# Moving operands, scalings and gates inside one decoder block: reused weight-block buffers, later output scaling, weight rows split behind the first tokens, and a gated projection that is parked before it is gated

## The chip, the cores and the metric

The kernel is one launch on one core of a Trainium2 chip. The core has a matrix engine (PE), a vector engine (DVE), a scalar engine (ACT), GpSimd (POOL), and sixteen DMA engines. SP issues most of the transfers. Every engine works through its own queue in a fixed order, and one that waits holds up all that stands behind it in that queue. The metric is the device time of one execution in microseconds (us). Three runs of the kernel before gave 1465.24 us in the median (1464.39 to 1468.95).

## The reference

The block takes x (1024 tokens by 1024 channels, float32). What matters here:

```
proj = x @ w_in -> q | f | i | og | pool_v | gate_a | gate_b
a = HGRN2(q, f, i), per-head RMSNorm, * g * sigmoid(og), @ w_a
b = per-group linear(causal_mean(pool_v) - pool_v) * pool_scale
mix = (sigmoid(gate_a) * a + sigmoid(gate_b) * b) @ w_out
x = LN(alpha * x + mix);  x = LN(alpha * x + relu(x @ w_up)^2 @ w_down)
```

HGRN2 is a recurrence over tokens with a forget gate f, eight heads of 128 channels. Its lower bound for f is made from `lb_logits` with a softmax over two rows. RMSNorm divides each head's output by the root of its mean square. The full float32 accuracy of the products is kept by splitting operands.

## The kernel before, in words

**Products.** Each operand is split into a high part (ACT casts it to the fast matrix format) and a low part (DVE subtracts the high part from the original). A product of two split operands is three matmuls. The large products use a seven-product scheme on 2 by 2 blocks (Strassen's, in Winograd's form): of a weight the blocks b11, b12, b21, b22 and the sums T1 to T4 are needed, of the tokens the blocks a11, a12, a22 and the sums s1 to s4. `pair` (line 267) issues seven steps. Each step prepares one weight operand (`w_part`, line 245, which casts on ACT, line 126, and subtracts on DVE, line 127) and then runs one product of twelve 128x512 matmuls (`prod`, lines 212 to 215). Operand tiles come from a ring of ten, that is, five operands ahead.

T3 = b22 - b12 (line 284), T2 = T3 + b11 (line 301), T4 = b21 - T2 (line 309), T1 = b22 - T2 (line 316). T3 has a tile of its own, `t`. T2 is written over b11, T1 over b12, T4 over b21. `loaded_blocks` (line 231) takes five tiles of a ring of six for each pair, in the order b11, b21, t, b12, b22, and issues the four loads on SP (line 223). So the next pair's b21 takes the buffer of this pair's b11, its b12 that of this pair's `t`, its b22 that of this pair's b12.

**First stage.** The value columns i of `w_in` are made first, from x as it arrives. `first_tokens("a11", ...)` (line 183) transposes x on PE, four row blocks kp of the operand, and splits them (line 131 on ACT, line 132 on DVE). `parts(b11)` (line 559) splits the four row blocks of the weight. The few instructions of the lower bound stand ahead of that (lines 440 to 449).

**Recurrence.** Sixteen halves (eight heads, two halves of the tokens) run as `turns` between the products of the other projections: after every product, one turn. A half has 8 or 9 turns (`PER_HALF`). In turn 0 `outputs` (line 1010) loads the sigmoid of og (tile `og`, one buffer, line 1012), makes the output in one PSUM bank, squares it on ACT (line 1022), takes the root (ACT, line 1023) and the reciprocal (DVE, line 1024), and at once scales four chunks on ACT (line 1026). At `TURN_BACK`, turn 4, `turn_outputs` transposes the scaled output, multiplies by og on DVE (line 1034) and sends it to DRAM: plain writes on SP (lines 636, 638) and writes that add, issued by GpSimd (line 640). `states` and the next load of v stand in the same turn.

**The projection by w_a.** Four column pairs p. In its first half (p = 0, 1) the operands `o` and `s` are loaded from DRAM (line 618) and split (lines 131, 132) while the products run. The second half (p = 2, 3) uses the split operands again. Each of the four results of a pair goes to a `take`: `gated` (line 1116) loads a gate tile (tag `ga`, twelve buffers) and a tile of b (tag `gb`, two buffers), multiplies (DVE, line 1120), adds (DVE, line 1121), and for p >= 2 splits the sum for the product by `w_out` (line 121); for p < 2 it is parked and split in the second half (`unpark`). Rows of `w_out` pass through `gb` too (line 1146). Then `mix` (line 1227) multiplies by `w_out`, normalises (GpSimd adds the last term, line 1199), and the MLP follows with the same `pair`.

**Order.** A planner lays down each queue's order ahead of the run, from program order, priorities and its own estimates of durations. During the recurrence PE keeps the program's order. `issue_after` puts the instructions of a block behind a named one on the same engine.

## Time and profile before

| What | Value |
| --- | --- |
| Median of three runs | 1465.24 us |
| The profiled execution | 1466.59 us |
| Its span, first to last instruction | 1464.9 us |
| PE, DVE, ACT, POOL busy | 1435.5, 1100.1, 759.0, 107.6 us |
| Mean granted PE clock | 0.996 |
| Moved by DMA | 228.15 MB, mean 156 GB/s |

Read it so. PE's records overlap, since matmuls are pipelined: a 128x512 matmul is recorded with about 0.39 us and yet they start about 0.23 us apart. So a stretch in which PE is "busy" throughout can be told from one that runs at full rate by counting matmuls. A row of the windows view has the stretch, its length, and for every engine busy time and number of instructions, then the granted clock, the DMA share and GB/s. In a timeline the bracket at the end of a row tells how long the engine sat idle before it and what ended that.

### The profile page before, as it was taken

Reading aid. Unit: us, or ns where it says so; the run is one execution under the profiler, and the core shown is the slowest. Engines: PE = TensorE matmul, PEld = TensorE weight load, DVE = VectorE, ACT = ScalarE, POOL = GpSimd, SP = SyncE. Lnnn points to the kernel's source line nnn. Section 1 sums busy time; section 2 is a strip of 40 time slices with the busy share of each in tenths; the row PEclk is TensorE's granted clock in tenths of the full one; section 3 lists DMA queues with packets and bytes.
Section 4 is the critical chain, followed back from the end, with each engine's and each line's share of the span. In section 5 each row is a group of like instructions: output and inputs, shape, how many; then the busy total and the mean of one; then the engine's idle time right before and its main releaser. Section 6 shows DMA issues by size and latency. Waiting matters only on the chain.

```text
span 1464.9 us, 20840 instructions
## 1 busy us (share of the span) xinstructions
PE 1435.5 (98%) x7377; PEld 1188.4 (81%) x7377; DVE 1100.1 (75%) x1807; ACT 759.0 (52%) x1383; POOL 107.6 (7%) x288
## 2 busy tenths in 40 slices
PE   8999999999999999999999999999999999999997
PEld 7788888788878888877788878888888888888886
DVE  4967886796797796477985598666666787777977
ACT  5545566655755655555542366555556443333435
POOL 0002011211211210000002100000000100000000
PEclk9999999999999999999999999999999999999999
DMA  7142245345435546788673135444447774445422
GB/s 259 58 137 87 73 126 169 80 134 155 109 87 146 142 116 184 211 300 286 204 232 113 61 99 180 144 154 148 157 148 261 280 262 142 166 132 170 129 72 115
DMA packets 187161, 228.15 MB, mean 156 GB/s; under 512 B 12176, under 2 KB 110512, under 8 KB 187056
## 3 DMA queue, kind: packets, MB, share of 16 engines
q1 hardware_dynamic: 181088, 212.91, 43.9%
q0 software_dynamic: 5184, 11.54, 4.0%
q10 hardware_dynamic: 784, 2.38, 0.5%
q8 instruction: 58, 0.95, 0.3%
q14 instruction: 47, 0.39, 0.1%
HBM read 149.70 MB, written 77.07 MB: 155 GB/s over the span
## 4 chain that ended last, share of the span: by engine, by line
PE 87%; DVE 6%; DMA 4%; issue 1%; ACT 1%; SPq 0%; DVEq 0%; POOL 0%; ACTq 0%
PE ps_pj L212 15%; PE ps_pj L215 14%; PE ps_pj L214 14%; PE ps_pj L1412 4%; PE ps_pj L1413 4%; PE ps_pj L1411 4%; PE ps_pj L114 2%; PE ps_pj L113 2%; PE ps_pj L115 2%; PE ps_tr L1412 1%; PE ps_tr L1413 1%; PE ps_tr L1411 1%; PE ps_sc L215 1%; DVE w L127 1%; PE ps_hg L215 1%
## 5 line engine op out<-in xcount | busy, mean ns | idle before, releaser
L212 PE MATMUL ps_pj<-act,w 128*128 128x512 f32 x1068 | 420.2, 395 | 10.8 <-ACT c L275 3.3
L215 PE MATMUL ps_pj<-act,w 128*128 128x512 f32 x1068 | 415.7, 391 | 1.3 <-DVE w L127 1.3
L214 PE MATMUL ps_pj<-act,w 128*128 128x512 f32 x1068 | 415.0, 390 | 0.0
L126 ACT CAST w<-raw 128x512 fp32r<-128x512 f32 x310 | 192.5, 622 | 278.1 <-PE ps_pj L214 201.7
L127 DVE TENSOR_TENSOR w<-raw,w 128x512 fp32r<-128x512 f32 x310 | 212.1, 686 | 92.8 <-ACT w L126 87.6
L212 PEld LDWEIGHTS ps_pj<-act,w 128*128 128x128 f32 x1068 | 200.7, 188 | 56.9 <-ACT c L275 4.6
L215 PEld LDWEIGHTS ps_pj<-act,w 128*128 128x128 f32 x1068 | 200.8, 188 | 45.2 <-DVE w L127 2.6
L214 PEld LDWEIGHTS ps_pj<-act,w 128*128 128x128 f32 x1068 | 200.8, 188 | 40.8 <-DVE act L132 0.2
L1373 ACT CAST act<-act 128x1024 fp32r<-128x1024 f32 x66 | 66.9, 1050 | 109.0 <-issue 35.0
L279 DVE TENSOR_TENSOR c<-c,ps_pj 128x512 f32<-128x512 f32 x95 | 64.8, 682 | 39.1 <-PE ps_pj L215 35.6
L1374 DVE TENSOR_TENSOR act<-act,act 128x1024 fp32r<-128x1024 f32 x66 | 79.5, 1220 | 18.5 <-ACT act L1373 17.4
L1413 PE MATMUL ps_pj<-act,act 128*128 128x512 f32 x240 | 93.0, 389 | 0.0
L1412 PE MATMUL ps_pj<-act,act 128*128 128x512 f32 x240 | 93.0, 389 | 0.0
L1411 PE MATMUL ps_pj<-act,act 128*128 128x512 f32 x240 | 92.5, 389 | 0.0
L275 ACT COPY c<-ps_pj 128x512 f32<-128x512 f32 x96 | 55.8, 581 | 3.1 <-issue 1.8
L284 DVE TENSOR_TENSOR raw<-raw,raw 128x512 f32<-128x512 f32 x43 | 29.6, 690 | 33.2 <-DMA raw<-in_w_in_dram 28.8
L1411 PEld LDWEIGHTS ps_pj<-act,act 128*128 128x128 f32 x240 | 45.0, 188 | 9.4
L1412 PEld LDWEIGHTS ps_pj<-act,act 128*128 128x128 f32 x240 | 45.0, 188 | 9.4
L1413 PEld LDWEIGHTS ps_pj<-act,act 128*128 128x128 f32 x240 | 45.0, 188 | 9.3
L1282 ACT ACTIVATE c<-c 128x512 f32<-128x512 f32 x61 | 38.5, 632 | 1.7
L1281 ACT ACTIVATE c<-c 128x512 f32<-128x512 f32 x46 | 29.1, 632 | 15.0 <-DVE c L279 15.0
L1367 DVE TENSOR_TENSOR act<-act,ps_pj 128x512 f32<-128x512 f32 x45 | 30.1, 682 | 6.0 <-PE ps_pj L1413 5.7
(416 smaller groups left out, 2680.5 us busy)
## 6 DMA issues: line engine op xcount, KB each, us to landing
h<-c SPq DMA_DIRECT2D x106, 256.0 KB, 2.7
raw<-in_w_in_dram SPq DMA_DIRECT2D x100, 256.0 KB, 3.3
act<-h SPq DMA_DIRECT2D x78, 256.0 KB, 3.0
draw<-in_w_down_dram SPq DMA_DIRECT2D x16, 1024.0 KB, 7.6
raw<-in_w_up_dram SPq DMA_DIRECT2D x56, 256.0 KB, 2.8
hf<-h SPq DMA_DIRECT2D x34, 256.0 KB, 3.0
s<-og POOLq DMA_DIRECT2D x28, 256.0 KB, 6.1
v<-v SPq DMA_DIRECT2D x16, 256.0 KB, 3.3
```

Source lines behind the costliest of these rows:

```text
L126: A.copy(hi, src)
L127: V.tensor_sub(lo, src, f(hi))
L212: PE.matmul(ps, wh[:, k], th, start=first and k == 0, stop=False, skip_group_check=True)
L214: PE.matmul(ps, wh[:, k], tl, start=False, stop=False, skip_group_check=True)
L215: PE.matmul(ps, wl[:, k], th, start=False, stop=k == CH - 1, skip_group_check=True)
L275: A.copy(t, ps)
L279: V.tensor_add(t, t, ps)
L1373: A.copy(hi, src)
L1374: V.tensor_sub(lo, src, f(hi))
L1411: PE.matmul(ps, hh[:, w], wh, start=fresh and n == 0, stop=False, skip_group_check=True)
L1412: PE.matmul(ps, hh[:, w], wl, start=False, stop=False, skip_group_check=True)
L1413: PE.matmul(ps, hl[:, w], wh, start=False, stop=n == M - 1, skip_group_check=True)
```

## The change

Five things are changed.

- In `pair`, T2 is written over b12 in place of b11, and T1 over T3's tile in place of b12.
- `outputs` stops at the reciprocal. The four scalings are issued two turns later (`scale_outputs`, `TURN_SCALE` = 2), behind the latest cast of a weight operand on ACT. `TURN_BACK` is 5, so `turn_outputs`, `states` and the load of v come one turn later.
- At the start only rows 0 and 1 of b11 are split ahead of the tokens. Row 2 is split behind the token block kp = 1, row 3 behind kp = 3, on both engines. The lower bound's instructions are issued behind the last split of a11.
- In the first half of the projection by w_a results are parked as they come (`park`), with no gate: the parked tiles are the rooms of the pair, eight buffers, and the fourth result is copied out of PSUM by ACT. Their gates and b tiles are loaded in the second half (`gate_parked`), u = 0 ahead of its first step, u = 1 behind it. `ga` has four buffers in place of twelve.
- The gating runs on GpSimd, but for the results that lie in PSUM (one per pair of the second half), which stay on DVE.

The diff, cut to its core:

```diff
 PER_HALF = 8.5
-TURN_BACK = 4
+TURN_BACK = 5
+TURN_SCALE = 2
...
-    made_last, made_hi = {}, {}
+    made_last, made_hi, made_kp = {}, {}, {}
...
         xp[name][kp] = act_tile()
-        made_last[name], made_hi[name] = (i.ins for i in split_into(xp[name][kp], src))
+        made_last[name], made_hi[name] = made_kp[name, kp] = [i.ins for i in split_into(xp[name][kp], src)]
...
+    last_hi = [None]
...
     def w_part(src):
-        return split(src, w_tile)
+        hi, lo = w_tile(), w_tile()
+        last_hi[0] = A.copy(hi, src).ins
+        V.tensor_sub(lo, src, f(hi))
+        return hi, lo
...
-    def pair(raw, rooms, takes, pz_tag="pj", twin=False, pc_tag="pj", turned=False):
+    def pair(raw, rooms, takes, pz_tag="pj", twin=False, pc_tag="pj", turned=False, into=None):
...
-        def added(t, ps):
-            V.tensor_add(t, t, ps)
-            return t
+        def added(t, ps, to=None):
+            to = t if to is None else to
+            V.tensor_add(to, t, ps)
+            return to
...
                 make_t2()
-            return w_part(b11)
+            return w_part(b12)
...
             if turned:
-                minus_sum(b11, c["t"], b11)
+                minus_sum(b12, c["t"], b11)
             else:
-                V.tensor_add(b11, c["t"], b11)
+                V.tensor_add(b12, c["t"], b11)
...
             if turned:
-                minus_sum(b21, b11, b21)
+                minus_sum(b21, b12, b21)
             else:
-                V.tensor_sub(b21, b21, b11)
+                V.tensor_sub(b21, b21, b12)
...
             if turned:
-                minus_sum(b12, b22, b11)
+                minus_sum(c["t"], b22, b12)
             else:
-                V.tensor_sub(b12, b22, b11)
-            return w_part(b12)
+                V.tensor_sub(c["t"], b22, b12)
+            return w_part(c["t"])
...
             with tc.high_priority(PRIO):
-                takes[0](added(c[11], ps["c"]))
+                takes[0](added(c[11], ps["c"], into and into()))
...
             with tc.high_priority(PRIO):
-                takes[1](ps["a"])
+                takes[1](copied(into, ps["a"]) if into else ps["a"])
...
         e01 = const.tile([P, 16], F32, name="e01")
-        V.tensor_max(lb, prm[:, 0:8], prm[:, 8:16])
...
-        V.tensor_scalar_mul(g_neg, g_col, -1.0)
...
         first_tokens("a11", "tr", "tr", "hg", "hg")
-        w = parts(b11)
+        w = parts(b11[:2])
+        for row, kp in zip(b11[2:], (1, 3)):
+            lo_done, hi_done = made_kp["a11", kp]
+            with tc.issue_after(lo_done), tc.issue_after(hi_done):
+                w += parts([row])
+        with behind_parts("a11"):
+            V.tensor_max(lb, prm[:, 0:8], prm[:, 8:16])
+            V.tensor_sub(e01[:, 0:8], prm[:, 0:8], lb)
+            V.tensor_sub(e01[:, 8:16], prm[:, 8:16], lb)
+            A.activation(e01, e01, AF.Exp)
+            V.tensor_add(lb, e01[:, 0:8], e01[:, 8:16])
+            V.reciprocal(lb, lb)
+            V.tensor_mul(lb, lb, e01[:, 0:8])
+            V.tensor_scalar(one_lb, lb, -1.0, 1.0, ALU.mult, ALU.add)
+            g_neg = e01[:, 0:8]
+            V.tensor_scalar_mul(g_neg, g_col, -1.0)
...
                 V.reciprocal(ss, ss)
-                for c in range(CH):
-                    A.activation(on[:, chunk(c)], o[:, chunk(c)], AF.Copy, scale=ss[:, c : c + 1])
+                self.o, self.root = o, ss
...
+            def scale_outputs(self):
...
+                with tc.issue_after(last_hi[0]):
+                    for c in range(CH):
+                        w = chunk(c)
+                        A.activation(self.on[:, w], self.o[:, w], AF.Copy, scale=self.root[:, c : c + 1])
...
                 for turn in range(1, round(at) - round(at - PER_HALF)):
+                    if turn == TURN_SCALE and old:
+                        old.scale_outputs()
...
         def mg_tile(tag, bufs):
-            return lambda: (pk[0] if tag == "ga" else mg).tile([P, HALF], F32, tag=tag, name=nm(tag), bufs=bufs)
+            return lambda: (pk[0] if tag in ("ga", "park") else mg).tile([P, HALF], F32, tag=tag, name=nm(tag), bufs=bufs)
...
-        def gated(j, u, park):
+        def gated(j, u, in_bank):
...
             def take(src):
-                t = loaded(gad[j][u], mg_tile("ga", 12))
-                V.tensor_mul(t, t, src)
-                V.tensor_add(t, t, loaded(pbd[j][u], mg_tile("gb", 2)))
-                if park:
-                    parked[u, j] = t
-                else:
-                    merged[u][j] = split_act(t)
+                eng = V if in_bank else G
+                t = loaded(gad[j][u], mg_tile("ga", 4))
+                eng.tensor_mul(t, t, src)
+                eng.tensor_add(t, t, loaded(pbd[j][u], mg_tile("gb", 2)))
+                merged[u][j] = split_act(t)
+            return take
...
+        def park(j, u):
+            def take(t):
+                parked[u, j] = t
...
                 raw[0], _ = wide_block(w_a, 0, cols[0], block_tile())
-            room = mg_tile("room", 4)
-            takes = [gated(2 * p + i, u, p < 2) for u in range(2) for i in range(2)]
-            return pair(raw, (c_tile, room, room), takes, "hg", True, turned=True)
...
-        def unpark(*which):
-            for u, j in which:
+            if p < 2:
+                room = mg_tile("park", 8)
+                takes = [park(2 * p + i, u) for u in range(2) for i in range(2)]
+            else:
+                room = mg_tile("room", 4)
+                takes = [gated(2 * p + i, u, (i, u) == (1, 0)) for u in range(2) for i in range(2)]
+            return pair(raw, (c_tile, room, room), takes, "hg", True, turned=True, into=room if p < 2 else None)
...
+        def gate_parked(u):
+            for j in range(CH):
+                t = parked[u, j]
+                G.tensor_mul(t, t, loaded(gad[j][u], mg_tile("ga", 4)))
+                G.tensor_add(t, t, loaded(pbd[j][u], mg_tile("gb", 2)))
...
+        def unpark(u):
+            for j in range(CH):
...
         two = [a_pair(p) for p in range(2, 4)]
-        then = (
-            lambda: unpark((0, 0), (0, 1), (0, 2), (0, 3)), lambda: out_rows_of(0, 1, 2, 3), lambda: out_rows_of(4, 5, 6, 7),
-            lambda: None, lambda: None, lambda: None, lambda: None,
-        )
-        for i, after in enumerate(then):
+        gate_parked(0)
+        for i in range(7):
             run(*(p[i : i + 1] for p in two))
-            after()
-        unpark((1, 0), (1, 1), (1, 2), (1, 3))
+            if i == 0:
+                unpark(0)
+                gate_parked(1)
+            elif i < 3:
+                out_rows_of(*range(4 * i - 4, 4 * i))
+        unpark(1)
```

More of the change, by code (lines that the diff above doesn't have):

```diff
@@ L439, in tile_hybrid_block @@
         e01 = const.tile([P, 16], F32, name="e01")
-        V.tensor_max(lb, prm[:, 0:8], prm[:, 8:16])
-        V.tensor_sub(e01[:, 0:8], prm[:, 0:8], lb)
-        V.tensor_sub(e01[:, 8:16], prm[:, 8:16], lb)
-        A.activation(e01, e01, AF.Exp)
-        V.tensor_add(lb, e01[:, 0:8], e01[:, 8:16])
-        V.reciprocal(lb, lb)
-        V.tensor_mul(lb, lb, e01[:, 0:8])
-        V.tensor_scalar(one_lb, lb, -1.0, 1.0, ALU.mult, ALU.add)
-        g_neg = e01[:, 0:8]
-        V.tensor_scalar_mul(g_neg, g_col, -1.0)
         x_rows = [xr.tile([P, CH, D], F32, name=f"x{u}", bufs=1) for u in range(2)]
```

## The prediction

> **What bounds the kernel now.** I read the page's busy times first, then the windows, then PE's waits, and then the timelines of the places at which PE stands.
>
> ```profile
> PE 1435.5 (98%) x7377; PEld 1188.4 (81%) x7377; DVE 1100.1 (75%) x1807; ACT 759.0 (52%) x1383; POOL 107.6 (7%) x288
> ```
>
> PE is the bound, and no part of the change takes a matmul away. All there is to win is PE's lost time: 1464.9 - 1435.5 = 29.4 us of recorded idleness, and some more inside "busy" stretches. The next rows show where. Columns: stretch, length, busy us and count for PE, PEld, DVE, ACT, POOL, then clock, DMA share, GB/s.
>
> ```profile
> 245.00:325.00 80.00, 76.76 (x524) 63.70 (x523) 65.09 (x137) 49.50 (x113) 14.68 (x43) 1.00 0.39 113
> 425.00:442.00 17.00, 14.24 (x117) 11.41 (x110) 16.97 (x39) 12.61 (x31) 3.98 (x13) 1.00 0.22 66
> 625.00:635.00 10.00, 7.17 (x24) 5.07 (x23) 5.32 (x9) 3.74 (x7) 0.00 (x0) 0.83 0.99 333
> 667.00:708.00 41.00, 37.74 (x162) 29.90 (x161) 31.08 (x51) 22.32 (x42) 0.00 (x0) 1.00 0.87 290
> 708.00:757.00 49.00, 48.75 (x215) 40.07 (x214) 42.69 (x71) 21.85 (x38) 0.00 (x0) 1.00 0.53 167
> ```
> ```profile
> 950.00:975.00 25.00, 25.00 (x112) 20.71 (x111) 16.28 (x25) 13.77 (x24) 0.00 (x0) 1.00 0.45 156
> ```
>
> The last row is the yardstick: a full stretch holds 112 matmuls in 25 us, one per 0.223 us. By it the first half of the projection by w_a (667 to 708) should hold 184 and holds 162: 22 x 0.223 = 4.9 us lost. Its second half (708 to 757) lacks 4.7, 1.0 us. The recurrence's two bad stretches have 3.24 + 2.76 = 6.0 us of idleness. The stretch from 625 lacks 21, 4.6 us, partly through a lower clock (0.83). The start comes below; the tail isn't touched.
>
> **The start.**
>
> ```profile
> 9.76 0.60 PE L170 MATMUL ps_hg<-ident,x 128*128 128x128 f32 x4
> 12.38 0.50 PE L501 MATMUL ps_pj<-w,act 128*128 128x512 f32 x1 [2.02 <-ACT act L131]
> ```
> ```profile
> 10.60 1.14 ACT L126 CAST w<-b 128x512 fp32r<-128x512 f32 x2 [2.12 <-DMA b<-in_w_in_dram]
> 11.64 0.21 ACT L443 ACTIVATE e<-e 128x16 f32<-128x16 f32 x1
> 11.76 1.05 ACT L131 CAST act<-ps_tr 128x512 fp32r<-128x512 f32 x2
> ```
>
> PE has transposed all four token blocks at 10.36, but the first product waits until 12.38 for the tokens' cast. ACT was free from 8.48 (10.60 less 2.12) and stood at the weight rows 2 and 3, whose load had not landed, with the tokens queued behind. With those rows and the exponential behind the tokens, ACT casts blocks 0 and 1 as soon as they are transposed. If PE's queue keeps the transposes ahead of the first product, that starts near 10.4: 2.0 us won. If it starts on block 0 at once, up to 3.2. Rows 2 and 3 are late next: cast from 10.6 on, while blocks 0 and 1 feed PE with 24 matmuls, 5.4 us, to 15.8. That covers two casts and subtractions (about 2.4 us). The ten small instructions of the lower bound go behind the split at no cost; what hides them is the whole first stage, as the first forget gate comes after it. I take -2.0, with ends at +0.5 (a row late once) and -3.2.
>
> **The scalings, two turns later.**
>
> ```profile
> PE ps_pj L212 <- ACT c L275: 3.3, 3, 1.6
> ...
> PE ps_hg L212 <- ACT act L131: 2.1, 1, 2.1
> ```
> ```profile
> 287.94 0.88 ACT L1026 ACTIVATE tH<-ps_hg,ss 128x128 f32<-128x128 f32 x3 [0.41 <-DVE ss L1024]
> 288.71 0.59 ACT L275 COPY c<-ps_pj 128x512 f32<-128x512 f32 x1
> ```
>
> PE's longest wait for a PSUM copy, 1.6 us, is this one: the copy stands on ACT behind three scalings, and these behind the reciprocal on DVE. Without them ACT is free at 287.53 (287.94 less 0.41), and the copy runs 1.2 us earlier. The work remains (four scalings per half, sixteen halves), with ACT at 49.50 of 80 us here. Who waits for it, the transposes, comes three turns later. I take -1.2 for this place and nothing for the others; ends 0 and -2.5, as DVE would be late next.
>
> **T2 over b12, and the turn that sends the output.** Both act on when the next pair's weights can be loaded.
>
> ```profile
> SPq L618 <- DMA s<-og: 50.1, 15, 7.6
> ```
> ```profile
> 277.18 0.34 SPq L618 DMA_DIRECT2D og<-og  x1
> 277.61 0.39 SPq L223 DMA_DIRECT2D raw<-in_w_in_dram  x1
> ```
> ```profile
> 273.91 0.69 DVE L127 TENSOR_TENSOR w<-raw,w 128x512 fp32r<-128x512 f32 x1 [1.07 <-ACT w L126]
> 276.63 0.69 DVE L127 TENSOR_TENSOR w<-raw,w 128x512 fp32r<-128x512 f32 x1 [2.03 <-ACT w L126]
> 280.79 0.69 DVE L284 TENSOR_TENSOR raw<-raw,raw 128x512 f32<-128x512 f32 x1 [3.46 <-DMA raw<-in_w_in_dram]
> ```
>
> DVE stands 3.46 us at T3 for the next pair's b22, and the recurrence's instructions queue behind it. That block's buffer was free at 274.60, when T1's low part (the row of 273.91) was done. But SP stood at the load of og, whose only buffer is read by the adding writes of the half before; this wait occurs 15 times, 50.1 us in all. The load of b22 went out at 277.61, 3.0 late.
>
> After the change b21's buffer is free as soon as T2 is made. b12 gets T3's tile, which now holds T1 to its end, 274.60; b22 gets b12's, free a little before. So both can go at 274.6 to 275.0: b12 later than before, b22 0.4 later than its old bound. By buffers alone T3 gains nothing. What decides is og. Its sending stands one turn later (one product of 12 x 0.223 = 2.7 us): PE's transposes, DVE's product, SP's plain writes, GpSimd's adding writes, the states (their first reader, the next output, comes three turns later) and the load of v. The old order had og's load between b12's and b22's, so the planner held its buffer to be free there. Moved by 2.7 us it should fall behind both. T3 then comes about 2.6 us earlier; with og still ahead, 2.7 later. DVE is full from 425 to 442 (16.97 of 17.00), so part of its waiting comes back on PE. Of the 6.0 us less 1.2 I take 2.0; ends -4.8 and +18.7 (worked out with its rival).
>
> **The first half of w_a, ungated.**
>
> ```profile
> ACT act L131 <- DMA c<-s: 7.3, 8, 2.2
> ACT act L131 <- DMA c<-o: 6.5, 3, 3.4
> ```
> ```profile
> DMA packets 8208, 11.67 MB, mean 292 GB/s; under 512 B 694, under 2 KB 3345, under 8 KB 8204
> ...
> ga<-ga SPq DMA_DIRECT2D x12, 256.0 KB, 5.3
> ...
> gb<-pb SPq DMA_DIRECT2D x4, 256.0 KB, 2.9
> ```
>
> These two views are of 667 to 707. ACT waits 13.8 us for operands from DRAM, and PE's 2.1 us wait above is one of them. Of the 11.67 MB moved, 16 loads of 262,144 bytes, 4.2 MB, are gates and b. At 292 GB/s they are 14.4 us of transfer, mixed into SP's queue between the operands. In the second half all of it meets a DMA share of 0.53. Here 8 products and 8 additions leave DVE, and two PSUM copies (0.59 us each, as the copy above) come to ACT at 22.32 of 41: no cost. Weights and ring waits stay, so of 4.9 us I take -4.0; ends -4.9 and 0.
>
> **The second half, with GpSimd.**
>
> ```profile
> 708.00:757.00 49.00, 7.43 (x11) 1.00 0.53 167
> ```
> ```profile
> 708.00:757.00 49.00, 7.31 (x11) 1.00 0.53 167
> ```
> ```profile
> L1199 POOL TENSOR_TENSOR r<-r,act 128x1024 f32<-128x1024 f32 x6 | 14.4, 2397 | 197.2 <-DVE r L1198 194.3 <-issue 2.9
> ```
> ```profile
> 257.64 0.19 POOL L922 COPY ek<-p 128x4 f32<-128x4 f32 x1
> ...
> 258.20 0.65 POOL L923 COPY ek<-p 128x4 f32<-128x4 f32 x1
> ```
>
> The first two rows are lines 1120 and 1121 alone: 11 multiplications and 11 additions, 14.7 us. Two results, four instructions, 2.7 us, stay on DVE, so it falls from 42.69 to 30.7 of 49. GpSimd gets 14 results, 28 instructions. Half of the 1024-wide row is 1.2 us each, 33.6 in all: it fits, barely. Behind it wait its own rings: 14 more b tiles and 8 rows of `w_out` pass through the two buffers of `gb`, and SP stands at each. The cover is `mix`, whose products for the first four row tiles PE can start on, and 16 of the 28 serve the later tokens. The last two rows are the same copy of four elements, 0.19 us and 0.65 us: GpSimd can be held up beside DVE. Whether DVE is held up by a long GpSimd instruction, no row shows. If it never is, the stretch wins at most its 1.0; if all 33.6 us exclude DVE, it has 64.3 us for 49, 15.3 over. The rows are nearer to GpSimd as the loser, so I take +0.5.
>
> The Trainium skill (SBUF — State Buffer, Who interferes with whom) says that a DVE instruction with two SBUF inputs and a GpSimd one that reads SBUF exclude each other, and that "Issue order, not op shape, decides who blocks." By that rule the 28 instructions may each hold DVE, which is the first rival below; the two copies agree with it from GpSimd's side.
>
> The stretch at 625 gets 0: b22's bound there is as before; ends -4.6 and +2.
>
> **The sum**, against the profiled execution of 1466.59 us (1464.9 us of span and 1.7 around it): -2.0 - 1.2 - 2.0 - 4.0 + 0.5 = -8.7, so 1457.9. The median of the runs stands 1.35 lower: 1465.24 - 8.7 = 1456.5.
>
> **Rivals.**
>
> *DVE is shut out in the second half.* For it: 33.6 us of GpSimd in 49, and the copy of 0.65 us. Against it: DVE falls to 63% there, and only 12 instructions are for the tokens that `mix` needs first. At half of the 15.3 over, +7.6 in place of +0.5: -1.6, 1463.6 us.
>
> *Slower: og's load still stands ahead of the weights.* One mechanism: the later turn frees og 2.7 us later at fifteen places, and T3 comes 2.7 later on DVE, with the recurrence behind it. At the place shown 3.46 us at T3 went with 1.6 us on PE, so 2.7 would cost 1.25, fifteen times 18.7. Then -2.0 - 1.2 + 18.7 - 4.0 + 0.5 = +12.0, 1477.2 us. It decides (slower by 4.4) from 11.1 us, 0.74 per place. Against it: DVE idles 15 of 80 us there, and a whole product has been added between.
>
> *The loads are only moved.* Operands still arrive late, since the weights of the second half and the buffers of `c` hold them, and the gates pile up on `gb`: -1.0 in place of -4.0, +1.0 in place of +0.5: -5.2, 1460.0. Against it: the 14.4 us of transfer stood right among the operands.
>
> *More than I count.* The low clock at 625 comes with the late weights there; if those come in time through the new order, 4.6 more go, and 2 more in the recurrence: -15.3, 1449.9.
>
> **How the numbers follow.** Forecast 0.50, DVE shut out 0.17, og ahead 0.15, only moved 0.10, more 0.08. A measurement of this kernel can tell about 0.3%, 4.4 us. Faster: 0.50 + 0.05 + 0.08 = 0.63. Within: 0.05 from "only moved", 0.13 from "shut out", 0.03 from og = 0.21. Slower: 0.12 + 0.04 = 0.16. The forecast's own range is 1451 to 1461. The range given, 1448 to 1469, leaves out og's case.
>
> **What would show it.** First product near 10.4. No scaling between a reciprocal and a PSUM copy; PE's wait for line 275 in the recurrence gone. SP's wait for og's writes well under 50 us, DVE's before line 284 shorter. No gate load before the second half, and over 178 matmuls in what answers to 667 to 708. GpSimd some 33 us busy in the second half, DVE's instructions still about 0.69 us and not set apart by gaps while GpSimd works. I am wrong if T3's waits grow, or if PE stands between the second half and `mix`.

## The result and the profile after

The changed kernel takes 1478.6 us in the median of four runs (1477.41 to 1479.8), beside 1465.1 us for the kernel before on the same chip. The ratio is 1.0091, 95% interval [1.0075, 1.0108]: 0.9% slower, where 0.6% faster was forecast, and outside the range. The profiled execution has a span of 1477.2 us, 12.3 more than before.

The page's busy times after, and the longest of PE's waits (what waited, on what, us in total, times, longest):

```profile
PE 1441.6 (98%) x7377; PEld 1193.3 (81%) x7377; DVE 1099.0 (74%) x1779; ACT 759.2 (51%) x1385; POOL 149.4 (10%) x316
```
```profile
PE ps_pj L213 <- ACT w L250: 7.0, 1, 7.0
PE ps_pj L213 <- ACT c L281: 5.9, 4, 2.3
PE ps_pj L114 <- DVE ga L1141: 3.3, 1, 3.3
```

The number of matmuls is the same. PE is idle for 35.6 us of the span, beside 29.4 before, and busy 6.1 us longer: half of the 12.3 us is waiting, and half is the same work at a lower pace. GpSimd has 42 us more, for 28 instructions. PE's longest wait is 7.0 us in one place, three times the longest before, and the wait for the PSUM copy in the recurrence, which was to go, has grown from 3.3 to 5.9 us. Where the time is shows best in the windows view, by matmul counts. Of before, the start and the two stretches around the projection by w_a:

```profile
0.00:15.00 15.00, 10.04 (x49) 8.84 (x50) 5.65 (x15) 6.92 (x13) 2.06 (x28) 0.94 0.86 291
15.00:30.00 15.00, 15.00 (x72) 12.51 (x71) 5.83 (x12) 9.30 (x18) 0.00 (x0) 0.95 0.87 306
600.00:675.00 75.00, 71.53 (x304) 57.24 (x303) 52.19 (x82) 38.35 (x68) 2.62 (x3) 0.98 0.84 272
675.00:775.00 100.00, 96.48 (x421) 78.25 (x420) 81.72 (x133) 45.31 (x81) 0.00 (x0) 1.00 0.73 239
```

and of after, with one of the prediction's stretches:

```profile
0.00:15.00 15.00, 12.64 (x63) 11.39 (x64) 6.07 (x14) 8.27 (x15) 2.06 (x28) 1.00 0.86 296
15.00:30.00 15.00, 14.55 (x77) 12.04 (x76) 9.29 (x18) 9.52 (x18) 0.00 (x0) 1.00 0.85 300
245.00:325.00 80.00, 75.44 (x513) 62.83 (x512) 64.13 (x136) 48.67 (x111) 13.80 (x43) 0.98 0.38 105
600.00:675.00 75.00, 67.17 (x280) 53.79 (x279) 47.87 (x77) 36.21 (x70) 2.65 (x3) 0.93 0.84 266
675.00:775.00 100.00, 93.02 (x391) 75.18 (x390) 75.69 (x97) 46.19 (x84) 43.55 (x28) 0.97 0.63 202
```

At 0.223 us a matmul: the start gained 140 - 121 = 19 matmuls, 4.2 us. From 600 to 675 it lost 24, 5.4 us; from 675 to 775 it lost 30, 6.7 us. That makes +7.9 of the 12.3. The stretches do not hold exactly the same work, since the kernel is shifted by some us, so this is a reading to within one or two us. The rest is in the recurrence, where PE idles 4.6 us from 245 to 325 (3.2 before) and the clock is lower. Note the clock column: 0.94 and 0.95 became 1.00 at the start, and 0.98 and 1.00 became 0.93 and 0.97 at the projection. That is where PE's longer work comes from. Apart from the last few us of the span, PE works 19.7 us at half the clock in this execution (five stretches, from 287, 434, 622, 693 and 769), and 6.8 us in the kernel before (two, from 13 and 631). Half of the difference is 6.4 us.

### The profile page after: what moved, and what is told of

Its sections match the earlier page's. It is cut to its first block, busy times and chain, and to the rows that moved or that the text cites. A ratio compares the mean times of both kernels' runs of the same rounds, so it can differ in the third digit from the quotient of the medians.

```text
span 1477.2 us, 20892 instructions
## 1 busy us (share of the span) xinstructions
PE 1441.6 (98%) x7377; PEld 1193.3 (81%) x7377; DVE 1099.0 (74%) x1779; ACT 759.2 (51%) x1385; POOL 149.4 (10%) x316
## 4 chain that ended last, share of the span: by engine, by line
PE 78%; DMA 6%; DVE 6%; issue 5%; ACT 3%; POOL 2%; SPq 0%; DVEq 0%; POOLq 0%; ACTq 0%
PE ps_pj L213 12%; PE ps_pj L215 12%; PE ps_pj L216 12%; PE ps_pj L1446 4%; PE ps_pj L1447 4%; PE ps_pj L1445 4%; PE ps_pj L114 2%; PE ps_pj L115 2%; PE ps_pj L116 2%; PE ps_tr L1446 1%; PE ps_tr L1447 1%; PE ps_tr L1445 1%; PE ps_hg L213 1%; PE ps_hg L215 1%; PE ps_sc L213 1%
## 5 line engine op out<-in xcount | busy, mean ns | idle before, releaser
L250 ACT CAST w<-raw 128x512 fp32r<-128x512 f32 x303 | 188.0, 622 | 272.8 <-PE ps_pj L215 196.2
L291 DVE TENSOR_TENSOR raw<-raw,raw 128x512 f32<-128x512 f32 x43 | 29.6, 688 | 33.0 <-DMA raw<-in_w_in_dram 28.4
L652 POOL DMA_DIRECT2D s<-og x28 | 25.0, 1165 | 145.2 <-DVE og L1052 145.2
```

The source lines that it names most:

```text
L250: last_hi[0] = A.copy(hi, src).ins
```

## The experiments

Theories at this point: (1) the later turn makes the next weights, or the pooled blocks, late; (2) GpSimd's gates and DVE hold each other up; and against both, that the loads of gates and b, now through smaller rings, are what is late. All ratios are to the kernel before on the same chip.

| Kernel | Median, us | Ratio | 95% interval |
| --- | --- | --- | --- |
| start alone | 1460.76 | 0.9963 | 0.9951 to 0.9975 |
| T2 over b12 alone | 1466.96 | 1.0002 | 0.999 to 1.0013 |
| scalings and turn alone | 1479.79 | 1.0091 | 1.0075 to 1.0106 |
| w_a and gates alone | 1476.04 | 1.0065 | 1.0051 to 1.0079 |
| scalings, turn 4 | 1467.1 | 1.0009 | 1.0 to 1.0018 |
| turn 5, old scalings | 1481.6 | 1.0106 | 1.0091 to 1.0121 |
| gates, GpSimd 16 wide (most of the gating left out) | 1467.98 | 1.0015 | 1.0006 to 1.0025 |
| gates, all on DVE | 1464.2 | 0.9992 | 0.9983 to 1.0001 |
| states at 5, sending at 4 | 1467.89 | 1.0018 | 1.0008 to 1.0029 |
| turn 5, writes by GpSimd | 1477.2 | 1.008 | 1.0067 to 1.0093 |
| turn 5, product into tH | 1471.54 | 1.0036 | 1.0024 to 1.0048 |
| turn 5, both | 1475.22 | 1.0052 | 1.0033 to 1.0071 |
| turn 4, product into tH | 1469.62 | 1.0023 | 1.0012 to 1.0033 |
| turn 3 | 1469.87 | 1.0018 | 1.0007 to 1.0028 |
| turn 5 but the last at 4 | 1472.25 | 1.0054 | 1.004 to 1.0067 |
| start, gates on DVE | 1460.83 | 0.9966 | 0.9954 to 0.9979 |
| the same with T2 | 1462.1 | 0.9969 | 0.9953 to 0.9985 |
| all, turn 4, gates on DVE | 1463.27 | 0.9981 | 0.9972 to 0.999 |

### The four parts, each alone

Each of these four kernels is the one before with one part of the diff: the hunks of the start; those of T2, T4 and T1 in `pair`; those of `scale_outputs`, `TURN_SCALE` and `TURN_BACK`; those of `park`, `gated` and `gate_parked`.

> Only the start is changed: weight rows 2 and 3 behind the token blocks, the lower bound behind the split. Theory (the loss is the sum of parts that act where they stand): PE's lost time in the first 75 us, 10.0 us before and 5.9 with all changes, falls by about 4 us here too, and the whole time by 3 to 4.5 us. Rival (a lead won at the start is used up in the recurrence, which stands on other waits): first product equally early, whole time within 1.5 us of before.

> Only T2 over b12 and T1 over T3's tile. Theory (buffers alone move T3's inputs by 0.4 us, and the turn is what costs): within 2 us of before, PE's idle time from 245 to 325 us about 3.2 us as before. Rival (b12 coming 2.5 us later holds DVE at T3): 3 to 6 us slower, with DVE's idle time before the T3 line clearly over 33 us.

> Only the scalings two turns later and the output's turn one later. Theory (the later turn keeps buffers of the recurrence longer, and the loads behind them on SP come late): 6 to 10 us slower, with most of it at 575 to 650 us, where the last turns and the pooled products meet, and some at 250 to 325. Rival (that stall comes from T2's buffers or from the shift of the start): within 2 us of before.

> Only the projection by w_a: first half parked, gates in the second half, GpSimd. Theory (the two-buffer ring of the b tiles and GpSimd make the second half's end late, the first half wins nothing): 6 to 9 us slower, with a stall of some 3 us where mix waits for a gated tile. Rival (the second half is late only since the recurrence before it ended badly, with operands and SP behind): 2 us slower or less, or faster by up to 4 as forecast.

The start gained 5.0 us by the medians, T2 nothing, scalings with the later turn cost 14, the projection's part 10. So two parts carry the loss; I had expected 6 to 10 and 6 to 9 us of them. All four add up to +20, the whole change to +13.5: the parts disturb each other.

The start's trace, PE's timeline:

```profile
9.68 0.60 PE L170 MATMUL ps_hg<-ident,x 128*128 128x128 f32 x4
10.04 0.48 PE L491 MATMUL ps_pj<-w,act 128*128 128x512 f32 x1
```
```profile
0.00:15.00 15.00, 12.36 (x63) 11.12 (x64) 5.87 (x14) 8.23 (x15) 2.06 (x28) 1.00 0.85 294
15.00:30.00 15.00, 14.55 (x78) 12.04 (x77) 9.33 (x18) 9.50 (x18) 0.00 (x0) 1.00 0.86 302
```

The first product stands right behind the last transposes, at 10.04 in place of 12.38. That is 2.3 us. Up to 30 us PE has 20 more matmuls than before, 4.5 us. Most of the other 2.2 us is clock: 0.94 and 0.95 before, 1.00 now. Before, the clock is 0.50 from 13.1 to 16.5, where matmuls start 0.43 us apart; that costs 1.7 us. Before, PE waited twice (1.3 us for x, 2.0 for the tokens' cast); here only once, 1.0 us for x. The Trainium skill (TensorE: Matmul & The Clock Gate, Part 1) says that PE falls to half rate after an idle window of about 3.4 us. The two waits of before come to 3.3 us with only transposes between them, so the rows do not contradict it; which window it was they do not show.

### Scalings or turn?

```diff
-TURN_BACK = 5
+TURN_BACK = 4        # scale_only: the part above with the old turn
```
```diff
-TURN_BACK = 4
+TURN_BACK = 5        # back5_only: kernel before with nothing else
```

> Kernel before with the four scalings moved behind the weight cast of the second turn, the sending of the outputs left at its old turn (4). The two edits of this part together made the kernel 14 us slower. Theory A, the later sending does it (og's buffer comes free a turn later, so the weights behind it are late): this run is between -2.5 and +2 us of before, since only the scalings moved. Theory B, the scalings do it (they now stand on ScalarE behind a cast that itself waits for a load, and the turning of the output waits for them): this run is 8 to 14 us slower. Theory C, it takes both (the scalings fit neither before nor behind the copies): in between.

> Kernel before with the sending of the outputs one turn later (5 in place of 4), the scalings where they were. Theory A, the later sending does it: 8 to 14 us slower, with vector engine waits at T3 or ScalarE waits at the weight cast longer at many of the halves. Theory B, the scalings do it: within 3 us of before. By the order of the queue, if og's load now goes out behind the two weight loads, the single stall of 3.46 us at T3 near 280 should be shorter; if ahead, near 6 us.

The turn does it all: +15.5 us by itself. The scalings are worth +1.3 us, at the edge of what can be measured. And they did not move. ACT's timeline with the scalings two turns later, at the old turn:

```profile
288.18 0.88 ACT L1038 ACTIVATE tH<-ps_hg,ss 128x128 f32<-128x128 f32 x3 [0.41 <-DVE ss L1030]
288.94 0.59 ACT L281 COPY c<-ps_pj 128x512 f32<-128x512 f32 x1
```

The reader is to see the same picture as before: three scalings, then PE's copy. In the whole change it is the same, at 285.82. What releases them is DVE's reciprocal, which stands in DVE's queue behind T3, the scans and a mask; in each of the sixteen halves, here as in the kernel before and in the whole change, the first scaling starts within 0.5 us of the reciprocal's end. A place two turns further on in the program, behind a cast that had already run, was no later place in the queue.

### What in the later turn costs 15 us

```diff
-                    if turn == TURN_BACK:
-                        if old:
-                            old.turn_outputs()
+                    if turn == TURN_BACK - 1 and old:
+                        old.turn_outputs()       # late_states, TURN_BACK = 5
+                    if turn == TURN_BACK:
```
```diff
-            nc.sync.dma_start(out=od[h][u], in_=t)
+            nc.gpsimd.dma_start(out=od[h][u], in_=t)     # back5_pool; osd likewise
```

> The later turn (5 in place of 4) was 15.5 us slower by itself. Here only half of what moved with it is late: the states, the load of v and the piece of the next half's preparation that takes their place are as in that kernel, while the transposes of the output, its product and its writes stay at turn 4. Theory A, the late sending does it (SP stands at og's plain write until the product, with the next weights' loads behind it in its queue): this kernel is within 3 us of before. Theory B, the states or the changed order of the pieces does it: 12 us or more slower.

> Kernel before with the sending, the states and the load of v all at turn 5, but the plain writes of the output issued from GpSimd's queue in place of SP's. Theory A (SP stands at og's write, the weights' loads behind it): most of the 15.5 us goes; what is left is the one stall near 624, where the loads of the pooled blocks wait for the buffers of tH that the outputs now hold longer (some 4 us): 0 to 6 us slower than before. Theory A2, the wait for og's buffer counts as well (og's load still waits for its writes): about 8 us slower. Theory B, states and pieces: 12 us or more slower.

With the states and v late and the sending at its old turn, 2 us are left: the sending does it. With the writes in GpSimd's queue 11.7 us remain, between what I had expected of two theories (about 8, and 12 or more). Two places in the traces show what the later sending does. First, near 250. SP's queue and DVE's T3, before:

```profile
240.07 0.34 SPq L636 DMA_DIRECT2D o<-og  x1
...
249.47 0.43 SPq L223 DMA_DIRECT2D raw<-in_w_in_dram  x1
```
```profile
253.68 0.69 DVE L284 TENSOR_TENSOR raw<-raw,raw 128x512 f32<-128x512 f32 x1 [1.65 <-DMA raw<-in_w_in_dram]
```

and with turn 5 alone:

```profile
243.75 0.34 SPq L636 DMA_DIRECT2D o<-og  x1
244.18 0.38 SPq L709 DMA_DIRECT2D og<-c  x1
244.61 1.53 SPq L638 DMA_DIRECT2D s<-og  x3
246.24 1.61 SPq L223 DMA_DIRECT2D raw<-in_w_in_dram  x2
...
250.22 0.47 SPq L223 DMA_DIRECT2D raw<-in_w_in_dram  x1
```
```profile
255.59 0.69 DVE L284 TENSOR_TENSOR raw<-raw,raw 128x512 f32<-128x512 f32 x1 [2.83 <-DMA raw<-in_w_in_dram]
```

The plain writes of the output fall 3.7 us later, and the first of the next weights' loads, whose buffer is free at 244.3 (DVE's subtraction of 243.64, 0.68 us long), now stands behind the four writes of the output and one other transfer: 1.9 us late. T3 too comes 1.9 us later, and the recurrence's scans stand behind it, but that load is not what it waits for. It waits for b22's, the last in each fence, which goes out 0.2 us behind the subtraction that frees its buffer in both kernels (249.47 and 250.22, subtractions done at 249.31 and 250.05). So 0.75 us are there already at the subtraction; the other 1.2 are the transfer, which lands 4.1 us after its issue before and 5.3 us after it now, with the transfers ahead of it more closely packed. It is not og's load that stands ahead of the weights, as the rival had it, but og's writes; yet over the whole recurrence DVE's waits for weights at T3 come to 30.1 us with turn 5 alone, beside 28.8 before, so T3's waits are not where the 15.5 us come from.

The order that I had forecast did come about. At the place that the prediction shows, near 280, SP's queue and DVE of the whole change:

```profile
270.04 2.21 SPq L224 DMA_DIRECT2D raw<-in_w_in_dram  x2
276.89 0.34 SPq L630 DMA_DIRECT2D og<-og  x1
```
```profile
277.96 0.69 DVE L291 TENSOR_TENSOR raw<-raw,raw 128x512 f32<-128x512 f32 x1 [3.39 <-DMA raw<-in_w_in_dram]
```

og's load stands behind both loads of weights, and still DVE waits 3.39 us at T3, beside 3.46 before. The later of the two loads goes out at 271.88, right behind the subtraction that frees its buffer (done at 271.85), and takes 6.0 us to land, where the load that T3 waited for before took 3.1. From 272 to 277.9 the queue of GpSimd's adding writes fills 50.7% of the DMA engines' time; from 277.6 to 280.7 in the kernel before it moves nothing. So what og's load had waited for, the adding writes, now runs beside the weights. That it slows them is my reading of these rows; no run here tests it alone. With turn 5 alone the order is the same there: T3's wait is 2.54 us, and T3 comes 2.4 us later than before.

Second, near 620, where the pooled blocks `po` are loaded into tH's two buffers, which hold the scaled outputs until PE has turned them. Before (PE, SP, ACT):

```profile
607.74 0.60 PE L1032 MATMUL ps_tr<-ident,tH 128*128 128x128 f32 x4
```
```profile
610.22 0.37 SPq L618 DMA_DIRECT2D tH<-po  x1
```
```profile
614.57 0.62 ACT L126 CAST w<-tH 128x512 fp32r<-128x512 f32 x1 [3.83 <-DMA tH<-po]
```

and with turn 5 alone (PE, SP, ACT, and the windows from 625):

```profile
618.82 0.60 PE L1032 MATMUL ps_tr<-ident,tH 128*128 128x128 f32 x4
```
```profile
619.79 0.39 SPq L223 DMA_DIRECT2D raw<-in_w_in_dram  x1
...
620.82 0.38 SPq L223 DMA_DIRECT2D raw<-in_w_in_dram  x1
...
621.97 0.41 SPq L618 DMA_DIRECT2D tH<-po  x1
```
```profile
629.65 0.62 ACT L126 CAST w<-tH 128x512 fp32r<-128x512 f32 x1 [10.04 <-DMA tH<-po]
```
```profile
625.00:630.00 5.00, 0.00 (x0) 0.00 (x0) 0.00 (x0) 0.35 (x1) 0.00 (x0) 0.79 1.10 277
630.00:635.00 5.00, 4.16 (x10) 3.21 (x11) 3.16 (x5) 2.31 (x5) 0.00 (x0) 0.53 1.03 368
```

The block's load had gone out 2.5 us behind the transposes, ahead of the weights; now it goes out 3.2 us behind, with two weight loads ahead of it, and takes 7.7 us to be used in place of 4.4, at a full DMA share. ACT, which casts in order, stands 10 us, and PE 5.9. Then the clock falls to 0.53, and in the next 5 us PE, busy for 4.16, starts 10 matmuls where that time at full rate holds 18.7: 1.9 us more. By the same section of the Trainium skill (TensorE: Matmul & The Clock Gate, Part 1) a wait over its window of about 3.4 us halves the clock; this row agrees, and the wait of 1.6 us near 287 in the kernel before left the clock at 1.00. But in the whole change a shorter wait, alone, goes before the half clock too (PE, and the window behind):

```profile
287.23 0.78 PE L213 MATMUL ps_pj<-act,w 128*128 128x512 f32 x1 [2.25 <-ACT c L281]
```
```profile
287.28:290.69 3.41, 3.41 (x8) 2.73 (x9) 3.41 (x11) 1.96 (x6) 0.10 (x1) 0.50 0.27 75
```

So do waits of 1.80 us (to 432.8) and 2.11 us (to 692.9) in the same execution, while one of 2.13 us (to 689.3) in the kernel before leaves the clock at 1.00. A wait well under 3.4 us can therefore cost 3.4 us at half the clock; when it does, these runs do not show.

How much is each place?

```diff
-                    if turn == TURN_BACK:
+                    if turn == (5 if n < 16 else TURN_BACK):     # back5_early, TURN_BACK = 4
```

> Kernel before with the sending at turn 5 for all halves but the last, which stays at turn 4. In the traces 7.1 us of PE's extra lost time under the later turn came after 600, most of it one stall of 5.9 us and the low clock behind it, where the load of a pooled block waits until the last outputs are transposed out of tH. If that one place is half of the price, this kernel is 7 to 9 us slower than before. If the places are independent of the last half's turn and the price is spread, 12 us or more; if the last place is all of it, within 3 us.

+6.6 us by the medians, +7.9 by the ratio (turn 5 alone: 15.7 and 15.5). So the last half's turn alone takes some 8 to 9 us, and the fifteen before it 7 to 8, about half a us each. But the place near 620 is eased in this kernel, not mended. The transposes are back at 615.19, and the block's load still goes out at 619.82, since SP stands 3.6 us, until 619.41, at a load of f that waits for a write; ACT stands 9.4 us, PE 3.4 in place of 5.9, and 3.4 us at half the clock follow in place of 6.8. So the release of tH is one part of that place, and SP's other waits are another.

The other question is whether the buffer of og, or SP's standing at its writes, is the price:

```diff
-                V.scalar_tensor_tensor(self.og, pt, gain, self.og, ALU.mult, ALU.mult)
-                put_output(self.h, self.u, self.og)
+                V.scalar_tensor_tensor(self.on, pt, gain, self.og, ALU.mult, ALU.mult)
+                put_output(self.h, self.u, self.on)     # on5 at turn 5, on4 at turn 4, on5_pool with GpSimd's writes
```

> Kernel before with the later turn (5), the output's product written into the tile of the scaled outputs (tH) in place of og's own, so that og's buffer is free when the product is made and not when its writes have landed; SP still stands at the plain write ahead of the weights' loads. Of the 15.5 us of the later turn, GpSimd's queue for the plain write took back 4. If og's buffer is the rest, this kernel comes to +4 to +8 us; if neither (tH and the order of the loads), it stays at +11 to +16, or gets worse, since tH is now held for longer.

> The same with the plain writes issued from GpSimd's queue as well, so that neither SP's place at the write nor og's buffer can hold the weights' loads. If these two are the whole cost of the later turn, it is within 3 us of before, and SP's wait for og's writes (50 us in before) is nearly gone. If more than 8 us remain, the cost is elsewhere: tH's buffers and the loads of the pooled blocks behind them near 620, or transfers that now run at the same time as the weights.

> Control: the product into tH's tile at the old turn (4). SP's wait for og's writes should shrink from 50 us to a few. If that wait costs something in the kernel before (the 3.46 us of the vector engine at T3 near 280), 2 to 5 us faster than before; if it is only a symptom, within 2 us.

> The sending, the states and the load of v one turn earlier (3 in place of 4). If a turn in the queue has a price by itself (og's writes ahead of the weights' loads, og's buffer), an earlier turn gains: 2 to 8 us faster. If PE now waits for the scaled outputs, which come late on ScalarE, or if the planner's order falls as badly as at 5: 3 us or more slower.

With the product in tH's tile the turn costs 5.3 instead of 15.5 us, as expected if og's buffer is most of the rest, and against its own control at turn 4 (+3.4) only 1.9, with intervals that overlap. The stretch 600 to 675 with turn 5 alone, and with the product in tH's tile:

```profile
600.00:675.00 75.00, 65.81 (x280) 52.75 (x279) 44.70 (x71) 36.24 (x71) 2.63 (x3) 0.93 0.78 247
```
```profile
600.00:675.00 75.00, 69.83 (x301) 55.35 (x300) 51.09 (x81) 38.77 (x71) 2.62 (x3) 1.00 0.88 278
```

The 21 more matmuls there are 4.7 us, about half of what is recovered (the profiled execution with the product in tH is the fastest of its eleven, 3.0 us under their median). So og's buffer matters at turn 5. It matters near 620 as well, where tH is now held for longer than with turn 5 alone and PE's wait is only 2.4 us: og is also one of the tiles into which the pooled stage splits its weights, and in the kernel before DVE stands 2.3 us for og's adding writes there, at 620.52. How much of that place is og and how much tH, these runs do not part. Writes by GpSimd took back 4 of 15.5; with the product in tH they took back nothing (+7.6 beside +5.3, intervals overlapping): SP's standing at the write is not a price that can be taken off by itself. With writes by GpSimd and the product in og's own tile, the wait only moved to og's load, from 48.7 us with turn 5 alone:

```profile
SPq L618 <- DMA s<-og: 65.4, 15, 8.8
```

The control says most about the prediction. At turn 4, with SP's wait for og's adding writes gone altogether, the kernel is 0.23% slower, not faster. That wait of 50.1 us, on which my forecast rested, was in the main a symptom: most of what SP got to earlier could not go earlier. Its waits at the weights' loads for DVE, which frees their buffers, grew from 282.5 to 316.5 us, and DVE's waits at T3 fell only from 28.8 to 26.9 us. It was not worth nothing: in this trace PE idles 2.2 us from 250 to 325 and 1.1 from 400 to 450, beside 3.2 and 2.8. But that gain and more goes in one place, a wait of 6.1 us at 616, with 6.8 us at half the clock behind it (283 matmuls from 600 to 675, beside 304). One turn earlier also gains nothing. Why the planner's order falls so in the control, and why the early turn and the late states cost 2 to 3 us, was not settled; each gives it another order in every queue.

### GpSimd or the loads?

```diff
-                G.tensor_mul(t, t, loaded(gad[j][u], mg_tile("ga", 4)))
+                n = 16      # gates_narrow; the addition and gated() likewise
+                G.tensor_mul(t[:, :n], t[:, :n], loaded(gad[j][u], mg_tile("ga", 4))[:, :n])
```
```diff
-                eng = V if in_bank else G
+                eng = V     # gates_on_dve; gate_parked() likewise
```

> The part with the parked half and GpSimd alone (10 us slower), with all loads and waits as there, but the 28 GpSimd instructions 16 columns wide in place of 512 (so most of the gating is left out). Theory A, GpSimd and the vector engine hold each other up: the 8 to 11 us lost between 725 and 800 go nearly all, vector engine instructions come back to 0.69 us, and the kernel is 2 to 5 us faster than before. Theory B, the gates' and b's loads through the small rings come too late: the loss stays at 7 to 11 us in that stretch.

> The same part with all 32 gate instructions of the second half on the vector engine, complete. Without GpSimd beside it an instruction takes 0.69 us; the 28 add 19 us to some 31 us of other work of the vector engine in 49 us, 50 in all: no slack. Theory A, GpSimd and the vector engine hold each other up: less than the 10 us lost with GpSimd, about +1 to +5 us. Theory B, the loads: the waits at the rings stay, and the vector engine now queues behind them: 10 us or more slower.

All gates on DVE bring the part from +10.3 to -1.7 us by the medians, where I had expected +1 to +5 for want of room on DVE; that it is faster than the kernel before is within the noise. The groups view from 700 to 775 (line, engine, operation, count, busy us, mean ns), of the part with GpSimd and then with DVE alone:

```profile
L127 DVE TENSOR_TENSOR w<-raw,w 128x512 fp32r<-128x512 f32 x13 | 11.7, 909 | 0.0
L181 DVE SCALAR_TENSOR_TENSOR raw<-raw,raw 128x512 f32<-128x512 f32 x6 | 8.3, 1415 | 0.0
```
```profile
L127 DVE TENSOR_TENSOR w<-raw,w 128x512 fp32r<-128x512 f32 x13 | 8.9, 681 | 0.0
...
L181 DVE SCALAR_TENSOR_TENSOR raw<-raw,raw 128x512 f32<-128x512 f32 x6 | 3.9, 679 | 0.0
```

The same 13 instructions take 909 ns in place of 681, the same six 1415 in place of 679. With GpSimd's instructions 16 wide they take 689 and 684 (in that kernel's `gated` the load of b also stands ahead of the product). In the whole change one sees a single case, on DVE and on GpSimd:

```profile
733.25 0.67 DVE L286 TENSOR_TENSOR c<-c,ps_pj 128x512 f32<-128x512 f32 x1
...
746.23 1.78 DVE L251 TENSOR_TENSOR w<-raw,w 128x512 fp32r<-128x512 f32 x1
```
```profile
731.03 3.45 POOL L1171 TENSOR_TENSOR park<-park,gb 128x512 f32<-128x512 f32 x2
...
745.74 1.71 POOL L1142 TENSOR_TENSOR ga<-ga,gb 128x512 f32<-128x512 f32 x1
```

The subtraction at 746.23 is done 0.56 us behind the end of GpSimd's instruction (747.45), less than the 0.68 that it takes alone: it stood until about then. The addition at 733.25, wholly beside GpSimd but with one operand in PSUM, takes its usual 0.67. GpSimd's own take 1.29 us when they are alone, many of them up to 1.80, and one 2.29 (at 707.68). The Trainium skill (SBUF — State Buffer, Who interferes with whom) has it that a DVE instruction with two SBUF inputs and a GpSimd one that reads SBUF exclude each other, and that one with at most one SBUF input, outside the two-port modes, does not contend; both halves of that agree with these rows.

GpSimd is not the whole of it: 16 wide, the part is still 2.1 us slower than before, where I had expected it 2 to 5 us faster, and 3.8 slower than DVE alone. There it is one wait of PE, 3.8 us, with 6.8 us at half the clock behind it, and a chain of GpSimd and ACT:

```profile
PE ps_pj L212 <- ACT room L275: 3.8, 1, 3.8
```
```profile
732.93 0.22 POOL L1125 TENSOR_TENSOR ga<-ga,gb 128x16 f32<-128x16 f32 x1 [5.89 <-DMA gb<-pb]
```
```profile
733.19 1.25 ACT L120 CAST act<-ga 128x512 fp32r<-128x512 f32 x2 [2.48 <-POOL ga L1125]
```

A tile of b comes through the ring of two, behind rows of `w_out`; GpSimd waits for it, ACT's cast of the gated result for GpSimd, and the PSUM copy for the cast. With DVE the planner put these elsewhere, and PE has no wait over 1.2 us there. So of the 12.0 us between GpSimd and DVE some 8 go with the width of GpSimd's instructions (their own length and what they hold up on DVE, which these runs do not part), and some 4 with the ring and the order; both with the low clock that follows the waits.

The windows of the part with all gates on DVE:

```profile
667.00:708.00 41.00, 40.50 (x177) 32.75 (x176) 36.22 (x59) 24.37 (x44) 0.00 (x0) 1.00 0.75 250
675.00:775.00 100.00, 99.50 (x436) 81.27 (x436) 81.74 (x132) 45.97 (x82) 0.00 (x0) 1.00 0.73 238
```

The first half has 177 matmuls for 162, 3.3 us, and from 675 to 775 PE idles 0.5 us.

### What is worth keeping

> The new order at the start together with the parked first half, all gates on the vector engine. The parts alone: -5.0 and -1.7 us. If the two stretches do not touch each other the sum is -6.7 us, 1459 us; if the earlier start only shifts the stalls that follow, about -5 us or less.

> The same with T2 over b12. That part alone came to +0.3 us, with a little less lost in the recurrence and a longer single stall at 615. If it is neutral here too: within 1.5 us of the kernel without it. If the planner's order of the loads changes with it: up to 5 us either way.

> The whole change with its two costly pieces taken back: the sending at turn 4, and the gates of the second half on the vector engine. By the parts alone it is -5.0 (start), -1.7 (parked half, gates on the vector engine), +0.3 (T2) and +1.3 (scalings), so 5 us faster than before, 1461 us. If the parts disturb each other, as the planner's order may: 1463 to 1467.

These are the parts' hunks put together, with the gates on DVE; the last is the whole change with `TURN_BACK = 4` and the gates on DVE. All three beat both kernels, but none beats the start alone. The start with the gates on DVE stands at 0.9966 and the start alone at 0.9963: the 1.7 us of the parked half are not seen beside it. The last is 2.4 us faster than before, where the parts alone add up to 5: they disturb each other here too. The more of the change is put in, the less is left: 0.9969 with T2, 0.9981 with the scalings too. The intervals still touch, so this order is a tendency.

## Why the prediction was wrong, point by point

- **The start, -2.0.** Right in mechanism, first product at 10.08 (forecast: near 10.4). Mis-sized: it is worth 5.0. I priced the wait and not the clock that goes with it: the windows of the first 30 us, with their 0.94 and 0.95, are not in my working. The same holds for the loss: the sum has no term for a clock that a new wait brings down, and that is half of the 12.3 us.
- **The scalings, -1.2.** Failed: measured +1.3. The step "ACT is free at 287.53, and the copy runs 1.2 us earlier" supposed that they leave their place. The bracket in the quoted row names their releaser, the reciprocal, and they still run right behind it.
- **T2 over b12, and the later turn, -2.0 together.** T2 alone is worth 0, within 1.9 us. The turn failed with the wrong sign, +15.5. "Moved by 2.7 us it should fall behind both" came true at the place shown. The step that failed is the next, "T3 then comes about 2.6 us earlier": the load went out when its buffer was free and landed 6.0 us later in place of 3.1, and DVE waited 3.39 us at T3, beside 3.46. og's load was the wrong thing to look at; SP's wait for og's writes was to fall "well under 50 us" and is 48.1 in the whole change. And the move has a price that I put at nothing: it delays og's writes and the release of og and tH, 7 to 8 us over fifteen halves, by waits that the runs do not part, and 8 to 9 us by the last half, where the pooled blocks' loads come late, the low clock included. I named tH's tile nowhere, though the row of the scalings shows it as their output.
- **The slower rival** gave 1477.2 and the kernel came to 1478.6, but not by its mechanism. T3's waits for weights did not grow in total (28.8 us in 16 before, 28.4 in 14 after), og's load fell behind the weights at the place shown, and the control at the old turn gains nothing on the whole. That the numbers lie close is luck.
- **The first half, -4.0.** Right in mechanism: 3.3 us there with the gates on DVE, of which the whole part keeps 1.7. In the change itself little of it is seen: 667 to 708 holds 161 matmuls, where over 178 were forecast for what answers to it. The early gates, GpSimd's among them, still ran into it: between 660 and 705 six gates and four tiles of b are loaded, against the forecast of none.
- **The second half, +0.5.** Failed. "The rows are nearer to GpSimd as the loser": both lose. That was my first rival, at +7.6; GpSimd costs 12.0 us against the same gates on DVE, some 8 of them with the width of its instructions, as that rival named. My row for the bound was a copy of four elements, and I weighed it over the mechanism. The cover I named was right in the other direction: DVE had the room, 32 gates fit without loss.
- **The stretch at 625, 0.** Wrong: it became the place of the largest single loss, a wait of 7.0 us with 10.2 us at half the clock behind it.
- **The warning signs** at the end of the prediction held: PE stands between the second half and `mix` (3.3 us for DVE line 1141, which waits for a gate's load), and DVE's instructions were lengthened.

## What to carry to other kernels

Before an operation is moved in program order, look at what releases it and what its tiles are used for next: the scalings could not move, and the turn was late for a buffer that another stage waits for. A long wait in a queue (SP's 50 us) is worth something only if the transfers behind it are able to go earlier, land earlier and are needed earlier; take it away in one run before counting on it. Offloading two-input work from a vector engine with room to GpSimd can cost more than it moves.

## What was not expected of the hardware

Waits of PE are often paid twice: one of 5.9 us was followed by 5 us at a clock of 0.53 (1.9 us more), three of 1.8 to 2.3 us by 3.4 us at half the clock each, and at the start 2.3 us of wait taken away brought 4.5 us of matmuls. A 128x512 addition or multiplication on GpSimd takes 1.29 us alone, under twice DVE's 0.69, but side by side DVE's two-input instructions go up to 1.78 and GpSimd's to 1.80 and once 2.29, so that two engines together did little more than one.
